# A two-layer diffusion step on one core: 43 lo halves of the first feed-forward's weights made by adding transfers, and three modulation units moved from TensorE to VectorE

## The chip, the cores and the metric

The kernel runs on one core of a Trainium2 chip. The metric is the device time of one execution in microseconds (us). The kernel before was timed three times: 2304.15, 2304.75 and 2308.19 us, median 2304.75 us. A further execution was profiled.

## The reference, cut to what matters

Two groups of 128 tokens with 2048 features (a context group and a latent group, so 256 columns in all) pass through two layers with shared weights. Each layer is a mixer and a gated feed-forward, and each of these is preceded by a modulated normalisation:

```
for l in range(2):
    mod = silu(cond) @ w_ada[l] + b_ada[l]          # six vectors of 2048 per layer and group
    sh1, sc1, gt1, sh2, sc2, gt2 = split(mod, 6)
    h = rmsnorm(x, g_norm_mix[l]) * (1 + sc1) + sh1
    x = x + gt1 * mixer(h)                           # l = 0: MLA + GQA, l = 1: differential attention
    h = rmsnorm(x, g_norm_ffn[l]) * (1 + sc2) + sh2
    x = x + gt2 * ((silu(gate) * val) @ w_down)      # gate, val: width-3 convolution of h @ w_up
y = rmsnorm(x, g_final)
```

All of it is float32. `w_up` is 2048 x 11264 and `w_down` 5632 x 2048 in each layer.

## The kernel before, in words

**Products.** Features lie on partitions and the 256 tokens on columns. Each 128 x 128 block of a weight is split into a hi part (rounded to the matmul's `fp32r` format) and a lo part (what the rounding left), and so are the activations. Three matmuls per block, hi by hi, hi by lo and lo by hi, add up in PSUM (`gemm`). A weight tile `raw` of 16 blocks, 128 x 2048 and 1 MB, comes by one DMA from SyncE's queue into one of three buffers (`Weights.load`). `split` then makes its two halves: ScalarE copies a half tile (128 x 1024) to `wh` (L248) and VectorE subtracts, giving `wl` (L249). There are four buffers of each, so the splits run up to four half tiles ahead of TensorE.

**Feed-forward** (`ffn`). It runs in two halves q. Each half has 44 up products of 16 blocks (one weight tile each), whose convolution ScalarE and VectorE do out of PSUM, and then 16 down products of 22 blocks, which are added to `x` on VectorE (L843). The first three up products are made ahead of it, in `modulated`.

**Modulation units.** `w_ada[l]` is cut into units (l, j, q): layer, one of the six vectors, a quarter of 512 columns. A unit can be worked in three ways. Units of the table `ROWS` are row sums on TensorE: four 1 MB tiles `araw`, 16 matmuls of 512 columns into the PSUM tile `ada` (`sum_rows`, L110), then a copy to `am` on ScalarE, four transposes (L113) and a few small VectorE instructions (`ada_finish`). In the trace each of those float32 matmuls has two records. Units of `FEATS` are eight steps on VectorE (`feature_step`, L473): each multiplies half of a loaded `araw` by a broadcast condition row and sums it; one 1 MB load serves two steps. Units of `DEEP` are done on VectorE beside the second mixer's attention in smaller pieces (L525).

**Pacing.** `pump` is called once per product. It adds the stage's rate for rows and for features to a balance and issues steps while the balance allows. `FRATE` holds the feature steps per product in up and down, and `RLIMIT` and `FLIMIT` hold how many units of the two tables may be begun by the end of each stage (`ab`, `ffn0`, `c`, `ffn1`). The instructions then go through a scheduler that sets each engine's order; some are pinned in program order (`keep_order`).

**Stages.** The first mixer runs until about 475 us, the first feed-forward (`ffn0`) until about 1163 us, the second mixer with its output projection until about 1580 us, and then the second feed-forward. In the second mixer each of eight heads has six products and its attention; row sums sit in the middle of a product, two tiles at a time.

Of the kernel before, what the change touches and what calls it, by code (L numbers as in the profile page):

```python
# [11 lines left out]
F32 = mybir.dt.float32  # L12
# [6 lines left out]
P = 128  # L19
# [35 lines left out]
FRATE = {"up": 0.7, "down": 1.42}  # L55
# [24 lines left out]
ROWS += [(1, 2, 1), (1, 2, 2), (1, 2, 3), (1, 4, 0), (1, 3, 0)]  # L80
FEATS = [(0, 5, 1), (0, 5, 2), (0, 5, 3)]
FEATS += [(1, j, q) for j in (1, 0) for q in range(4)]
FEATS += [(1, 2, 0)]
FEATS += [(1, 5, q) for q in range(4)]
DEEP = [[(0, 3, q) for q in range(4)], [(1, 4, q) for q in range(1, 4)] + [(1, 3, q) for q in range(1, 4)]]
RLIMIT = {"ab": 16, "ffn0": 17, "c": 22, "ffn1": 22}
FLIMIT = {"ab": 0, "ffn0": 12, "c": 12, "ffn1": 16}
# [7 lines left out]
def step_kernel(ctx: ExitStack, tc: tile.TileContext, A: dict):  # L95
# [157 lines left out]
    class Weights:  # L253
# [3 lines left out]
        def __init__(self, src, nblk, per_tile, cycle=0):  # L257
            self.src, self.nblk, self.per = src, nblk, per_tile
            self.cycle = cycle
            self.at, self.blocks, self.tiles = 0, [], []  # L260
            self.half = None
            self.begun = []
            self.used = lambda: None

        def load(self, parts=1, pin=lambda i: i):
            n = self.per
            if self.cycle:
                n = min(n, self.cycle - self.at * n % (-(-self.cycle // n) * n))
            n *= self.nblk if self.per < TB else 1
            raw = T_(wpool, [P, 4, 512], "raw").rearrange("p g n -> p (g n)")  # L270
            w = n * P // parts
            for i in range(parts):
                s = slice(i * w, (i + 1) * w)
                pin(sp.dma_start(out=raw[:, s], in_=self.src[self.at, :, s]))
            self.at += 1
            return raw, n
# [4 lines left out]
        def take(self):  # L281
            return self.begun.pop(0) if self.begun else self.load()

# [20 lines left out]
        def chunk(self):  # L304
            while len(self.blocks) < self.nblk:
# [3 lines left out]
                raw, n = self.take()  # L309
                n0 = FINE if fine[0] else 8  # L310
                for lo in range(0, n, n0):
                    hi = min(lo + n0, n)
                    w = (hi - lo) * P
                    if lo % 8 == 0:
                        wh_ = T_(wpool, [P, 1024], "wh", F32R, bufs=4)
                        wl_ = T_(wpool, [P, 1024], "wl", F32R, bufs=4)
                    at = lo % 8 * P
                    wh, wl = wh_[:, at:at + w], wl_[:, at:at + w]
                    split(wh, wl, raw[:, lo * P:hi * P])
# [1181 lines left out]
    def ffn(hx, W, ready, turn, l, st):  # L1501
# [16 lines left out]
        with tc.tile_pool(name=f"ffn{l}", bufs=1) as fp, banks(f"pffn{l}") as pf:  # L1518
# [25 lines left out]
            def up(q):  # L1544
                gs = []
                for i in range(q * KQ, (q + 1) * KQ):
                    rate = 0 if i < LATE else FRATE["up"]
# [14 lines left out]
            def down(gs, q):  # L1562
# [4 lines left out]
                for c in range(KD):  # L1567
# [13 lines left out]
                    pump(0, 0 if quiet else FRATE["down"])  # L1581
                return u

            for q in range(NQ):
                gs = up(q)
# [195 lines left out]
```

## Time and profile before

| | before |
|---|---|
| three timed runs | 2304.15, 2304.75, 2308.19 us (median 2304.75) |
| profiled execution, own time | 2307.52 us |
| its span | 2305.7 us |
| TensorE busy / weight loads busy | 2275.9 / 2182.1 us |
| VectorE / ScalarE / GpSimd busy | 1885.6 / 1195.7 / 188.1 us |
| read from HBM | 609.32 MB |

Times inside the profile count from the start of the span. Busy time of TensorE overlaps from matmul to matmul, so its pace is read from the starts of successive weight loads (PEld), one per matmul. The profiled execution's own time is 1.8 us over its span and 2.8 us over the median of the timed runs.

### The profile page before, as it was taken

Reading aid. Unit: us, or ns where it says so; the run is one execution under the profiler, and the core shown is the slowest. Engines: PE = TensorE matmul, PEld = TensorE weight load, DVE = VectorE, ACT = ScalarE, POOL = GpSimd, SP = SyncE. Lnnn points to the kernel's source line nnn. Section 1 sums busy time; section 2 is a strip of 40 time slices with the busy share of each in tenths; the row PEclk is TensorE's granted clock in tenths of the full one; section 3 lists DMA queues with packets and bytes.
Section 4 is the critical chain, followed back from the end, with each engine's and each line's share of the span. In section 5 each row is a group of like instructions: output and inputs, shape, how many; then the busy total and the mean of one; then the engine's idle time right before and its main releaser. Section 6 shows DMA issues by size and latency. Waiting matters only on the chain.

```text
span 2305.7 us, 47484 instructions
## 1 busy us (share of the span) xinstructions
PE 2275.9 (99%) x19496; PEld 2182.1 (95%) x19496; DVE 1885.6 (82%) x2973; ACT 1195.7 (52%) x1959; POOL 188.1 (8%) x238
## 2 busy tenths in 40 slices
PE   8999999999999999999999999999999999999998
PEld 6788878999999999999999999999999999999998
DVE  4667979989999999999978988898899965666654
ACT  4345555665553355555575455457555434555543
POOL 0002111300000000001130001023000000000011
PEclk9999999999999999999999999999999999999999
DMA  9987888777777777777788888776667755555553
GB/s 376 367 343 293 326 311 338 288 277 264 262 255 291 291 272 260 272 258 258 288 293 293 318 322 310 267 268 229 246 256 262 264 200 189 199 191 194 198 189 126
DMA packets 100122, 617.15 MB, mean 268 GB/s; under 512 B 10752, under 2 KB 18880, under 8 KB 33344
## 3 DMA queue, kind: packets, MB, share of 16 engines
q1 hardware_dynamic: 99904, 614.11, 72.2%
q8 instruction: 153, 2.51, 0.4%
q14 instruction: 65, 0.53, 0.1%
HBM read 609.32 MB, written 4.75 MB: 266 GB/s over the span
## 4 chain that ended last, share of the span: by engine, by line
PE 93%; DVE 3%; DMA 2%; issue 1%; POOL 1%; ACT 1%; SPq 0%; DVEq 0%; ACTq 0%; POOLq 0%
PE acc L110 86%; PE ada L110 3%; PE att L110 2%; DVE wl L249 1%; DVE hx L525 1%; DMA more<-w_ada 1%; PE att L113 1%; DMA raw<-w_out_c 0%; PE misc L110 0%; DMA araw<-w_ada 0%; DMA kvb<-w_ada 0%; POOL dev L807 0%; PE ada L113 0%; DVE rope L858 0%; ACT wh L248 0%
## 5 line engine op out<-in xcount | busy, mean ns | idle before, releaser
L110 PE MATMUL acc<-hx,wh 128*128 128x256 f32 (+1 forms) x7264 | 1255.2, 278 | 4.2 <-ACT wh L248 1.7
L248 ACT CAST wh<-raw 128x1024 fp32r<-128x1024 f32 (+1 forms) x834 | 796.6, 967 | 869.8 <-PE acc L110 736.6
L249 DVE TENSOR_TENSOR wl<-raw,wh 128x1024 fp32r<-128x1024 f32 (+1 forms) x834 | 925.4, 1126 | 246.9 <-ACT wh L248 240.2
L110 PEld LDWEIGHTS acc<-hx,wh 128*128 128x128 f32 x7264 | 1099.8, 188 | 23.2 <-ACT wh L248 8.1
L110 PE MATMUL acc<-hx,wl 128*128 128x256 f32 (+1 forms) x3632 | 1007.8, 278 | 5.3 <-DVE wl L249 5.1
L110 PEld LDWEIGHTS acc<-hx,wl 128*128 128x128 f32 x3632 | 684.5, 188 | 9.5 <-DVE wl L249 6.9
L110 PE MATMUL acc<-g,wh 128*128 128x256 f32 x2816 | 478.8, 276 | 0.0
L110 PEld LDWEIGHTS acc<-g,wh 128*128 128x128 f32 x2816 | 424.0, 188 | 0.0
L110 PE MATMUL acc<-g,wl 128*128 128x256 f32 x1408 | 388.1, 276 | 0.0
L473 DVE CUSTOM_DVE_ANT_0 junk<-araw,condb 128x2048 f32<-128x2048 f32 x128 | 294.4, 2300 | 0.0
L110 PEld LDWEIGHTS acc<-g,wl 128*128 128x128 f32 x1408 | 264.2, 188 | 0.0
L211 POOL TENSOR_TENSOR sqacc<-sqacc,sq 128x256 f32<-128x256 f32 x62 | 71.5, 1154 | 1491.1 <-ACT sq L207 1490.9
L110 PE MATMUL acc<-hxc,wh 128*128 128x256 f32 (+1 forms) x1056 | 189.3, 281 | 0.0
L110 PEld LDWEIGHTS acc<-hxc,wh 128*128 128x128 f32 x1056 | 161.9, 188 | 1.8 <-issue 1.7
L110 PE MATMUL acc<-hxc,wl 128*128 128x256 f32 (+1 forms) x528 | 146.9, 278 | 0.0
L110 PEld LDWEIGHTS acc<-hxc,wl 128*128 128x128 f32 x528 | 99.6, 189 | 0.2
L110 PE MATMUL acc<-wh,hxc 128*128 128x256 f32 (+1 forms) x512 | 95.0, 283 | 0.5 <-DVE nt L818 0.5
L1531 ACT ACTIVATE cv<-acc,convw 128x256 f32<-128x256 f32 x169 | 94.1, 557 | 0.0
L525 DVE CUSTOM_DVE_ANT_0 hx<-block,condb 128x1024 fp32r<-128x1024 f32 x65 | 79.3, 1221 | 7.3 <-DMA block<-w_ada 6.8
L1537 DVE SCALAR_TENSOR_TENSOR cv<-acc,convw,cv 128x254 f32<-128x254 f32 x169 | 81.1, 480 | 3.2
L843 DVE SCALAR_TENSOR_TENSOR x<-acc,mod,x 128x128 f32<-128x128 f32 x190 | 57.3, 344 | 31.6 <-PE acc L110 31.6
L110 PEld LDWEIGHTS acc<-wh,hxc 128*128 128x128 f32 x512 | 79.4, 188 | 3.4 <-issue 2.5
(263 smaller groups left out, 1800.4 us busy)
## 6 DMA issues: line engine op xcount, KB each, us to landing
raw<-w_up SPq DMA_DIRECT2D x176, 1024.0 KB, 4.8
araw<-w_ada SPq DMA_DIRECT2D x136, 1024.0 KB, 6.0
raw<-w_down SPq DMA_DIRECT2D x88, 1024.0 KB, 4.8
raw<-w_in_c SPq DMA_DIRECT2D x48, 1024.0 KB, 6.9
block<-w_ada SPq DMA_DIRECT2D x41, 512.0 KB, 6.8
raw<-w_in_ab SPq DMA_DIRECT2D x18, 1024.0 KB, 9.1
raw<-w_out_ab SPq DMA_DIRECT2D x16, 1024.0 KB, 7.9
raw<-w_out_c SPq DMA_DIRECT2D x16, 1024.0 KB, 7.1
```

The costliest lines, as they stand in the source:

```text
L110: return self.placed(nc.tensor.matmul(*a, **kw))
L113: return self.placed(nc.tensor.transpose(*a, **kw))
L211: eng.tensor_tensor(out=st["acc"], in0=st["acc"], in1=sq, op=ALU.add)
L248: pin(act.copy(out_hi, src))
L249: pin(dve.tensor_tensor(out=out_lo, in0=src, in1=out_hi.bitcast(F32), op=ALU.subtract))
L473: keep_order(dve.tensor_tensor_reduce(out=T_(feat["pool"], [P, D], "junk"), in1=feat["row"][:, c], in0=feat["raw"].rearrange("p g n -> p ( ...
L525: keep_order(dve.tensor_tensor_reduce(out=self.junk, in0=self.raw, in1=self.row[:, c].rearrange("p (g n) -> p g n", g=2), scale=1.0, scala ...
L843: dve.scalar_tensor_tensor(out=x[:, c, s], in0=ps[:, s], scalar=mod[:, l, 3 * which + 2, c, g:g + 1], in1=x[:, c, s], op0=ALU.mult, op1=AL ...
L1531: pin(act.activation(y, ps, AF.Identity, scale=cw[:, 1, m:m + 1], bias=cw[:, 3, m:m + 1]))
L1537: pin(dve.scalar_tensor_tensor(out=y3[:, :, :T - 1], in0=p3[:, :, 1:], scalar=cw[:, 2, m:m + 1], in1=y3[:, :, :T - 1], op0=ALU.mult, op1=A ...
```

## The change

Three `ROWS` units, (1, 2, 1), (1, 2, 2) and (1, 2, 3), become `FEATS` units, and `FLIMIT["ffn0"]` goes from 12 to 15, so that all three are worked in `ffn0`. `FRATE` becomes a list per layer, with higher rates for layer 0. In `ffn0`, `go_far` names a stretch of tiles for the up and the down weights of each q. `prepare`, called for each tile taken there, keeps two further tiles loaded and, where the tile's number leaves 1 or 3 when divided by 5, makes its second half at once in buffers of its own, two of each kind: ScalarE writes `farh` (hi) and `farl` = -hi, and GpSimd issues a DMA that adds the same 512 KB of the weight from HBM onto `farl`. No VectorE subtraction is made for such a half.

```diff
-FRATE = {"up": 0.7, "down": 1.42}
+FRATE = [{"up": 0.9, "down": 1.8}, {"up": 0.7, "down": 1.42}]
+LEAD = (9, 3)
-ROWS += [(1, 2, 1), (1, 2, 2), (1, 2, 3), (1, 4, 0), (1, 3, 0)]
+ROWS += [(1, 4, 0), (1, 3, 0)]
-FEATS += [(1, 2, 0)]
+FEATS += [(1, 2, q) for q in range(4)]
-RLIMIT = {"ab": 16, "ffn0": 17, "c": 22, "ffn1": 22}
-FLIMIT = {"ab": 0, "ffn0": 12, "c": 12, "ffn1": 16}
+RLIMIT = {"ab": 16, "ffn0": 17, "c": 19, "ffn1": 19}
+FLIMIT = {"ab": 0, "ffn0": 15, "c": 15, "ffn1": 19}
...
+        def go_far(self, home, start, stop, last):
+            self.far, self.until = home, stop
+            self.span = range(start, last)
+
+        def prepare(self):
+            while len(self.begun) < 2 and self.at < self.until:
+                self.begun.append(self.load())
+            for raw, n in self.begun:
+                i = next(i for r, i in self.index if r is raw)
+                if i in self.span and i % 5 in (1, 3) and not any(m[0] is raw for m in self.made):
+                    wh = T_(self.far, [P, 1024], "farh", F32R, bufs=2)
+                    wl = T_(self.far, [P, 1024], "farl", F32R, bufs=2)
+                    act.copy(wh, raw[:, 8 * P:n * P])
+                    act.activation(wl, wh.bitcast(F32), AF.Copy, scale=-1.0)
+                    pool.dma_start(out=wl, in_=self.src[i, :, 8 * P:n * P], accum_op=ALU.add)
+                    self.made.append((raw, wh, wl))
...
+                if self.far:
+                    self.prepare()
+                made = [m[1:] for m in self.made if m[0] is raw]
...
+                    if made and lo == 8:
+                        wh, wl = wh_, wl_ = made[0]
+                    else:
...
             for q in range(NQ):
+                if l == 0:
+                    at, n = 2 * KQ * q, KQ * KD // TB
+                    W.go_far(fp, at + LEAD[q], at + 2 * KQ, at + 2 * KQ)
+                    WD.go_far(fp, n * q + 3, n * q + n, n * q + n - 6 * q)
```

In the order of the changed program GpSimd's queue has 43 such transfers: 14 for the up and 8 for the down weights of the first half of `ffn0`, 16 and 5 for the second. On VectorE the feature steps in these four stretches go from 28, 19, 32 and 17 to 35, 26, 40 and 19.

The first place is TensorE in the second mixer, in the middle of a v product of a middle head. `acc` are the two PSUM tiles of the product, `ada` the one of the row sums. Before:

```order
L110 MATMUL acc_16556<-wh_16560,hxc_14392 128x256
L110 MATMUL acc_16557<-wh_16560,hxc_14392 128x256
L110 MATMUL acc_16557<-wl_16561,hxc_14392 128x256
L110 MATMUL acc_16557<-wh_16560,hxc_14392 128x256
L110 MATMUL ada_16183<-araw_16192,condw_79 32x512 x4
L110 MATMUL ada_16183<-araw_16297,condw_79 32x512 x4
L110 MATMUL acc_16556<-wh_16564,hxc_14392 128x256
L110 MATMUL acc_16556<-wl_16565,hxc_14392 128x256
```

And the same place in the changed program:

```order
L111 MATMUL acc_16658<-wh_16662,hxc_14510 128x256
L111 MATMUL acc_16659<-wh_16662,hxc_14510 128x256
L111 MATMUL acc_16659<-wl_16663,hxc_14510 128x256
L111 MATMUL acc_16659<-wh_16662,hxc_14510 128x256
L111 MATMUL acc_16658<-wh_16666,hxc_14510 128x256
L111 MATMUL acc_16658<-wl_16667,hxc_14510 128x256
```

The two rows of row sums are gone and the product goes on. Six such pairs of rows (48 matmuls) and three rows of four transposes leave TensorE's order after the first pumped unit, and no matmul joins it; elsewhere only the operands `wh` and `wl` of some become `farh` and `farl`.

The second place is ScalarE in `ffn0`, among the up products. `cv<-acc` empties the PSUM tile of a product, `wh<-raw` is the hi part of a half tile. Before:

```order
L248 CAST wh_6835<-raw_6833 128x1024
L248 CAST wh_6839<-raw_6833 128x1024
L1531 ACTIVATE cv_6755<-acc_6706,convw_2384 128x256
L248 CAST g_6693<-cv_6687 128x256
L248 CAST wh_6898<-raw_6896 128x1024
L1553 ACTIVATE cv_6755<-cv_6755 128x256
L248 CAST wh_6902<-raw_6896 128x1024
```

The changed program:

```order
L1557 ACTIVATE cv_6844<-acc_6795,convw_2384 128x256
L249 CAST wh_7000<-raw_6855 128x1024
L249 CAST wh_7063<-raw_6922 128x1024
L1557 ACTIVATE cv_6914<-acc_6865,convw_2384 128x256
L249 CAST g_6852<-cv_6844 128x256
L299 CAST farh_6991<-raw_6989 128x1024
L249 CAST wh_7067<-raw_6922 128x1024
L300 ACTIVATE farl_6992<-farh_6991 128x1024
```

The hi part and its negative for the second half of a later tile stand between the halves of the tile before it. TensorE's order uses `farl_6992` in the second half of product `acc_7140`, which comes after `acc_6865`, `acc_6928`, `acc_7004` and `acc_7071`. Over the 43 the product in question is most often the fourth after the last one emptied ahead of the negation, and at the least the third.

The third place is GpSimd's queue at the passage from the modulation of `ffn0` (`hx`, `block`) to what follows. Before:

```order
L807 TENSOR_SCALAR block_5444<-block_5444,scl_78,mod_77 128x128 x2
L811 TENSOR_TENSOR hx_5342<-block_5433,hx_5342 128x256
L811 TENSOR_TENSOR hx_5342<-block_5444,hx_5342 128x256
L211 TENSOR_TENSOR sqacc_12789<-sqacc_12789,sq_12878 128x256
L211 TENSOR_TENSOR sqacc_12789<-sqacc_12789,sq_12976 128x256
```

The changed program:

```order
L833 TENSOR_SCALAR block_5444<-block_5444,scl_78,mod_77 128x128 x2
L837 TENSOR_TENSOR hx_5342<-block_5433,hx_5342 128x256
L837 TENSOR_TENSOR hx_5342<-block_5444,hx_5342 128x256
L301 DMA farl_5957<-w_up 128x1024
L301 DMA farl_6099<-w_up 128x1024
```

The queue, which had nothing between the modulation and the sums of squares (`sqacc`) of the last down products, now holds the adding transfers there, 39 of them ahead of the first `sqacc` and the last four among those.

More of the change, by code (lines that the diff above doesn't have):

```diff
@@ L274, in load @@
                 pin(sp.dma_start(out=raw[:, s], in_=self.src[self.at, :, s]))
+            self.index.append((raw, self.at))
             self.at += 1
@@ L1546, in up @@
                 for i in range(q * KQ, (q + 1) * KQ):
-                    rate = 0 if i < LATE else FRATE["up"]
+                    rate = 0 if i < LATE else FRATE[l]["up"]
                     fine[0] = False
```

15 lines of the change are left out of this document (8 added, 7 removed).

## The prediction

> **What bounds the kernel now.** I read the page's busy times and chain first, then the chain in order of time, then the busy times by stage.
>
> ```profile
> PE 2275.9 (99%) x19496; PEld 2182.1 (95%) x19496; DVE 1885.6 (82%) x2973; ACT 1195.7 (52%) x1959; POOL 188.1 (8%) x238
> PE 93%; DVE 3%; DMA 2%; issue 1%; POOL 1%; ACT 1%; SPq 0%; DVEq 0%; ACTq 0%; POOLq 0%
> 474.80 690.47 PE acc L110 x6090
> ```
>
> TensorE sets the time: 93% of the chain is its own work, and the third row says that all of `ffn0` is one unbroken piece of 6090 matmuls, 690.47 / 6090 = 0.1134 us each. A product of 16 blocks (48 matmuls) is thus 5.44 us. Time is won here only by taking instructions off TensorE, and anything that makes it wait in `ffn0` is lost in full. The stages (columns: stretch, its length, busy us and instructions of each engine, granted clock, DMA share, GB/s):
>
> ```profile
> 475.00:600.00 125.00, 125.00 (x1104) 125.00 (x1103) 112.57 (x149) 70.25 (x96) 0.00 (x0) 1.00 0.70 251
> 600.00:722.00 122.00, 122.00 (x1079) 122.00 (x1078) 112.42 (x141) 60.34 (x78) 0.00 (x0) 1.00 0.72 266
> 722.00:842.00 120.00, 120.00 (x1062) 120.00 (x1060) 111.19 (x135) 50.88 (x56) 0.00 (x0) 1.00 0.79 294
> 842.00:1070.00 228.00, 228.00 (x2014) 228.00 (x2013) 210.61 (x278) 122.00 (x173) 1.59 (x2) 1.00 0.71 257
> 1070.00:1163.00 93.00, 93.00 (x823) 93.00 (x822) 91.42 (x129) 48.16 (x85) 15.96 (x13) 1.00 0.79 286
> 1300.00:1350.00 50.00, 50.00 (x421) 46.58 (x420) 46.85 (x77) 24.89 (x48) 4.86 (x6) 1.00 0.85 309
> 1350.00:1400.00 50.00, 50.00 (x419) 47.91 (x416) 38.59 (x65) 25.27 (x44) 2.33 (x4) 1.00 0.85 319
> 1400.00:1450.00 50.00, 50.00 (x427) 48.17 (x426) 46.07 (x85) 27.31 (x54) 4.17 (x6) 1.00 0.85 305
> 1450.00:1510.00 60.00, 58.97 (x487) 54.66 (x487) 49.89 (x95) 30.07 (x66) 7.24 (x9) 1.00 0.71 259
> ```
>
> VectorE is nearly as full as TensorE: in the five rows of `ffn0` it is idle for 688.0 - 638.2 = 49.8 us, in the first half's down products (722 to 842) for 8.8 us, in the last ones (1070 to 1163) for 1.6 us. So the three units don't fit there unless VectorE is given room, which is what the 43 halves do.
>
> **What is taken off TensorE.** The weight loads around one pair of row sums, in the middle of a v product, and the matmuls around one group of transposes:
>
> ```profile
> 1387.25 0.19 PEld L110 LDWEIGHTS acc<-wh,hxc 128*128 128x128 f32 x1
> 1387.56 0.16 PEld L110 LDWEIGHTS ada<-araw,condw 128*32 128x32 f32 x8
> 1388.02 0.13 PEld L110 LDWEIGHTS ada<-araw,condw 128*32 128x32 f32 x4 [0.30 <-issue]
> 1388.45 0.13 PEld L110 LDWEIGHTS ada<-araw,condw 128*32 128x32 f32 x4 [0.30 <-issue]
> 1389.42 0.19 PEld L110 LDWEIGHTS acc<-wh,hxc 128*128 128x128 f32 x1 [0.84 <-issue]
> 1434.31 0.60 PE L113 MATMUL ada<-cst,am 128*128 128x128 f32 x4
> 1434.74 1.48 PE L110 MATMUL att<-dk,dq 128*128 128x128 f32 x8
> L110 PEld LDWEIGHTS ada<-araw,condw x160: 106/109/110, 1172.3 to 1504.9; 128*32 128x32 f32 x160
> ```
>
> From the last load of the product to its next one are 2.17 us where 0.11 would do, so a pair costs 2.06 us, and four transposes cost 0.43 us. The last row has 160 loads in this stage, 16 for a pair: ten pairs, five units. The first unit is worked inside `modulated`, and the change only puts another in its place, the second is pumped as before, and six pairs and three groups of transposes go: 6 x 2.06 + 3 x 0.43 = **13.7 us**.
>
> What is late next there is VectorE, whose work in the second mixer stays. In the four late windows TensorE loses 4.1, 2.5, 2.5 and 4.5 us, and VectorE was idle for 3.2, 11.4, 3.9 and 10.1. Only the first goes below nothing, by about 1 us, and such a deficit is first drawn from the splits, which run ahead:
>
> ```profile
> ACT wh L248 <- PE acc L110: 100.6, 69, 3.7
> DVE on L1459 <- POOL var L1457: 7.6, 7, 3.0
> DVE drec L1428 <- ACT p L875: 6.8, 6, 1.8
> DVE hx L525 <- DMA more<-w_ada: 5.6, 4, 2.9
> ```
>
> These are waits between 1200 and 1510 us. ScalarE waited 69 times for TensorE to free a `wh`: all four half tiles were ready, 4 x 2.72 = 10.9 us of stock. Against that, part of VectorE's idle time is its own waits for the softmax and for pieces of `w_ada`, some 20 us, and cannot be filled. The bounds are 0 (the stock covers everything) and 6.6 us (the first and third window give back all they lose). I take 1.5 us, near the lower end, because of the 69 waits.
>
> **What is added in ffn0.** Costs from the groups of 500 to 720 us:
>
> ```profile
> L249 DVE TENSOR_TENSOR wl<-raw,wh 128x1024 fp32r<-128x1024 f32 x81 | 97.2, 1222 | 13.2 <-ACT wh L248 12.8
> L248 ACT CAST wh<-raw 128x1024 fp32r<-128x1024 f32 x82 | 86.4, 1055 | 107.5 <-PE acc L110 91.2 <-ACT g L248 12.4 <-issue 3.9
> L473 DVE CUSTOM_DVE_ANT_0 junk<-araw,condb 128x2048 f32<-128x2048 f32 x30 | 68.7, 2291 | 0.0
> L473 DVE DVE_READ_ACCUMULATOR2_ANT mod<- 128x1 f32 x30 | 4.3, 142 | 0.0
> ```
>
> VectorE gets 3 x 8 = 24 steps of 2.43 us (58.4) and loses 43 subtractions of 1.22 us (52.5): +5.9 us of 49.8. By stretch, with the counts of the order: up of the first half +7 steps, -14 subtractions, 0; its down +7, -8, **+7.2 us of 8.8**; up of the second half +8, -16, 0; its down +2, -5, -1.2. It fits everywhere, tightly in the first down. ScalarE gets 43 negations, bounded by a cast: 45 us of its 336 idle ones. Its PSUM emptying is delayed by one such instruction at most, with three PSUM tiles in turn. Cost on the path: nothing, and if VectorE's cover were gone, the 7.2 us of the first down.
>
> The trace has no adding transfer. The nearest rows for its duration are loads:
>
> ```profile
> raw<-w_up SPq DMA_DIRECT2D x176, 1024.0 KB, 4.8
> raw<-w_in_ab SPq DMA_DIRECT2D x2, 512.0 KB, 15.3
> ```
>
> 1 MB of `w_up` lands after 4.8 us, and the slowest row of the page, 512 KB in a full queue at the start, takes 15.3. The room: TensorE mostly uses `farl` in the second half of the fourth product after the one emptied last before the negation, 3.5 x 5.44 = 19.0 us later, of which ScalarE spends some 4.1 (emptying 0.6, the cast of g 0.4, three half tiles at 1.05); so 15 us are left, in the shortest case 9.5. From the nearest row, w_up's, I take about 5 us, hidden, cost 0; the other end stands under the first rival. GpSimd's queue holds nothing else until the sums of squares, and the twelve `w_ada` loads only move to an earlier stage of SyncE's queue.
>
> **Sum.** 13.7 - 1.5 + 0 = 12.2 us off. The profiled execution, 2307.52 us (span 2305.7), would become 2295.3; against the median of the runs, 2304.75, that is **2292.5, say 2293 us**.
>
> **The rivals.**
>
> (a) *The adding transfers land late*, on the other side. If one takes L us instead of the 15 there are, TensorE stands in the middle of a product, and the later splits only refill their four buffers meanwhile, so nothing is caught up: (L - 15) x 43. The gain is gone at L = 15 + 12.2 / 43 = 15.3 us, by chance what the slowest row above shows; at 16 us the time is 2293 + 43 = 2336. For it: such a transfer reads the target as well as the weight and is queued by GpSimd, and no row shows either. Against it: 5 us would have to become three times as many, on engines that are busy for 0.70 to 0.79.
>
> (b) *DMA is full in the first down.* There 294 GB/s take a share of 0.79, so 372 would fill it. The change brings 7 steps (3.5 loads, 3.7 MB) and 8 transfers (4.2 MB) into 120 us: 360 GB/s if a transfer counts once, 395 if the read of its target counts as much again. The second is 6% too much, 7.4 us, giving 2300. The other stretches stay below 355 even then. [...]
>
> (c) *GpSimd holds up VectorE* while it makes the transfers. The two do get in each other's way beside the sums of squares:
>
> ```profile
> L211 POOL TENSOR_TENSOR sqacc<-sqacc,sq 128x256 f32<-128x256 f32 x62 | 71.5, 1154 | 1491.1 <-ACT sq L207 1490.9
> L249 DVE TENSOR_TENSOR wl<-raw,wh 128x1024 fp32r<-128x1024 f32 x20 | 27.2, 1379 | 0.0
> ```
>
> The second row is from 1075 to 1160 us, where GpSimd works: 1379 ns against 1222. If each issue stopped VectorE for a `sqacc`'s 1.15 us, the stretches would get 16, 9, 18 and 6 us more, over their idle time by about 8, 1 and 3 in the last three: 12 us, back at 2305. [...]
>
> (d) *VectorE sets the second mixer* once the row sums are gone: the upper bound of 6.6 us, so a gain of 7.1 and 2298.
>
> That the change doesn't do what it says is excluded by the order of the instructions.
>
> **How the numbers follow.** Forecast 0.60; (a) 0.18, since only its price is large; (b) 0.08, (c) 0.06, (d) 0.08. A measurement of this kernel can tell about 0.2% from no change, 4.6 us, so faster means below 2300.1. The forecast and most of (d) lie there (0.66), (b), (c) and the rest of (d) are within it or just at its edge (0.13), and (a) with the worse ends of (b) and (c) is slower (0.21). The forecast's own range is 2290 (no give-back, 13.7 off, and a little scatter) to 2298. The range reaches from 2289 over (d), (b) and (c) to 2310, where only the late part of (a) and a little below are left out.
>
> **What would show it.** In the changed profile: the ten pairs of `ada` loads from 1172 to 1505 us become four, and the second mixer with its output projection is 12 us shorter; `ffn0` stays one piece of `acc` of about 690 us; TensorE has no wait for a DMA of `farl`, and that DMA lands in under 9.5 us; VectorE is busy for some 95% of `ffn0` and its `wl` keeps 1222 ns before 1070 us. A wait of PEld for `farl`, or for `raw` in the first down, would make (a) or (b) right; gaps before `wl` in the second mixer (d).

## The result, and the profile after

The changed kernel is **slower**: 2323.97 us (median of four runs, 2320.66 to 2326.57) against 2304.82 for the kernel before, timed beside it; the ratio is 1.0079, 95% interval 1.0062 to 1.0097. The forecast was 2293.0, and 2310.0 was the upper end of its range. The profiled execution took 2326.57 us, its span is 2324.8.

From the page of the changed kernel the busy times and the shares of the chain by engine, and from its chain in order of time the pieces of `ffn0`:

```profile
PE 2292.3 (99%) x19388; PEld 2209.0 (95%) x19388; DVE 1888.9 (81%) x2975; ACT 1231.6 (53%) x1999; POOL 227.8 (10%) x281
PE 94%; DVE 2%; DMA 2%; POOL 1%; ACT 1%; issue 0%; SPq 0%; DVEq 0%; ACTq 0%; POOLq 0%
```

```profile
473.16 205.57 PE acc L111 x1749
678.73 11.17 DMA farl<-w_up
689.95 505.71 PE acc L111 x4265
```

TensorE has 108 instructions less and is busy for 16.4 us more. The chain shows why: 505.71 / 4265 = 0.1186 us for each matmul, where the one piece of before had 0.1134. Only one DMA stands in the chain of `ffn0`, for the 11.17 us from its issue to its landing; TensorE stood still for 2.5 of them. The same is seen by stretch (columns as in the prediction); here the number of weight loads in a stretch of fixed length is what counts:

```profile
475.00:600.00 125.00, 125.00 (x1070) 125.00 (x1069) 110.22 (x144) 76.50 (x101) 7.13 (x8) 1.00 0.89 296
600.00:722.00 122.00, 119.81 (x1000) 119.58 (x999) 104.62 (x135) 64.37 (x84) 6.90 (x8) 0.99 0.87 292
722.00:842.00 120.00, 120.00 (x1018) 120.00 (x1017) 110.12 (x130) 52.72 (x55) 6.06 (x7) 1.00 0.94 333
842.00:1070.00 228.00, 228.00 (x1931) 228.00 (x1930) 204.14 (x263) 128.83 (x177) 12.98 (x15) 1.00 0.91 310
1070.00:1163.00 93.00, 93.00 (x790) 93.00 (x789) 89.66 (x120) 50.12 (x80) 17.65 (x15) 1.00 0.90 312
1520.00:1570.00 50.00, 50.00 (x427) 50.00 (x427) 50.00 (x84) 28.92 (x51) 14.98 (x10) 1.00 0.69 241
```

TensorE is busy without a gap in four of the five rows of `ffn0` at a granted clock of 1.00, and yet it does 3 to 4% less in these: 1930 loads in 228 us are 118.1 ns apart, 2013 before were 113.3. A busy share of 100% hid the loss. The last row is from the output projection behind the second mixer; there too 427 loads stand where the kernel before had 443:

```profile
1520.00:1570.00 50.00, 50.00 (x444) 50.00 (x443) 47.85 (x89) 29.83 (x60) 10.84 (x10) 1.00 0.69 237
```

The weight loads at the first use of a far half, some rows left out (start, duration, then the instruction; each row of `wh` or `farh` starts a block of three loads):

```profile
504.90 0.30 PEld L111 LDWEIGHTS acc<-hx,wh 128*128 128x128 f32 x2
505.24 0.30 PEld L111 LDWEIGHTS acc<-hx,wh 128*128 128x128 f32 x2
505.58 0.30 PEld L111 LDWEIGHTS acc<-hx,farh 128*128 128x128 f32 x2
505.93 0.31 PEld L111 LDWEIGHTS acc<-hx,farh 128*128 128x128 f32 x2
506.29 0.31 PEld L111 LDWEIGHTS acc<-hx,farh 128*128 128x128 f32 x2
...
508.09 0.31 PEld L111 LDWEIGHTS acc<-hx,farh 128*128 128x128 f32 x2
508.45 0.31 PEld L111 LDWEIGHTS acc<-hx,wh 128*128 128x128 f32 x2
...
511.98 0.19 PEld L111 LDWEIGHTS acc<-hx,wh 128*128 128x128 f32 x1
```

A block takes 0.34 us (113.3 ns a load) up to 505.58, then 0.36 (120 ns) while `farh` and `farl` are loaded; and when `wh` and `wl` follow, it does not go back: 511.98 - 508.45 = 3.53 us for ten blocks, 117.7 ns a load. That slow pace lasts to the end of `ffn0` (93.00 / 789 = 117.9 ns in the last stretch). In the second mixer both paces occur: right behind the kernel's pairs of wider matmuls (`PUSH`) it is the fast one 9 times out of 14, and the output projection is slow again (50.00 / 427 = 117.1 ns).

To compare kernels, three numbers are read from the starts of weight loads. **ffn0** is the stretch from the last load for the moving operand `u` (the last up product made ahead, in `modulated`) to the last for `g` (its second down products); **second mixer** goes from there to the last load for `hxc`, which is the same place ahead of the second feed-forward. In `ffn0`, a gap over 0.25 us counts as a **wait** (less 0.113), and the **pace** is the mean of all other gaps, some 6200. The numbers come from one profiled execution of each kernel, whose own time lies up to 4.3 us from the median of its runs (e6), so differences of two or three us between them can be scatter.

| | before | after | difference |
|---|---|---|---|
| ffn0, us | 702.4 | 734.4 | +32.0 |
| of it waits, us (number) | 0 | 2.5 (1) | +2.5 |
| pace, ns | 113.36 | 118.13 | 6195 x 4.77 ns = +29.5 |
| second mixer, us | 433.2 | 422.1 | -11.1 |
| all else, us | 1170.1 | 1168.3 | -1.8 |
| span, us | 2305.7 | 2324.8 | +19.1 |

Of the 1.8 us, 1.6 lie ahead of `ffn0`, whose start, 458.6 us here and 460.2 before, scatters between 457.9 and 460.8 in the profiles of this study (all but e3's).

### The profile page after: what moved, and what is told of

Same layout as the page of the kernel before. It is cut to its first block, busy times and chain, and to the rows that moved or that the text cites. A ratio compares the mean times of both kernels' runs of the same rounds, so it can differ in the third digit from the quotient of the medians.

```text
span 2324.8 us, 47335 instructions
## 1 busy us (share of the span) xinstructions
PE 2292.3 (99%) x19388; PEld 2209.0 (95%) x19388; DVE 1888.9 (81%) x2975; ACT 1231.6 (53%) x1999; POOL 227.8 (10%) x281
## 3 DMA queue, kind: packets, MB, share of 16 engines
q0 software_dynamic: 6192, 22.55, 5.3%
## 4 chain that ended last, share of the span: by engine, by line
PE 94%; DVE 2%; DMA 2%; POOL 1%; ACT 1%; issue 0%; SPq 0%; DVEq 0%; ACTq 0%; POOLq 0%
PE acc L111 89%; PE ada L111 3%; PE att L111 2%; DMA kvb<-w_ada 1%; DVE wl L250 1%; PE att L114 1%; DMA farl<-w_up 0%; PE misc L111 0%; DMA araw<-w_ada 0%; POOL dev L833 0%; DVE hx L551 0%; PE ada L114 0%; DVE x L1668 0%; POOL hxc L837 0%; ACT wh L249 0%
## 5 line engine op out<-in xcount | busy, mean ns | idle before, releaser
L111 PE MATMUL acc<-hx,wh 128*128 128x256 f32 (+1 forms) x6784 | 1188.8, 280 | 5.2 <-ACT wh L249 1.7
L249 ACT CAST wh<-raw 128x1024 fp32r<-128x1024 f32 (+2 forms) x791 | 749.7, 961 | 765.7 <-PE acc L111 637.4
L250 DVE TENSOR_TENSOR wl<-raw,wh 128x1024 fp32r<-128x1024 f32 (+2 forms) x791 | 876.3, 1121 | 264.6 <-ACT wh L249 260.8
L111 PEld LDWEIGHTS acc<-hx,wh 128*128 128x128 f32 x6784 | 1032.8, 189 | 24.0 <-issue 8.5
L111 PE MATMUL acc<-hx,wl 128*128 128x256 f32 (+1 forms) x3392 | 946.0, 279 | 4.7 <-DVE wl L250 4.4
L111 PEld LDWEIGHTS acc<-hx,wl 128*128 128x128 f32 x3392 | 639.5, 189 | 8.1 <-DVE wl L250 6.3
L111 PEld LDWEIGHTS acc<-g,wh 128*128 128x128 f32 x2608 | 396.6, 189 | 0.0
L499 DVE CUSTOM_DVE_ANT_0 junk<-araw,condb 128x2048 f32<-128x2048 f32 x152 | 349.5, 2299 | 1.3 <-DMA araw<-w_ada 1.3
L111 PE MATMUL acc<-hx,farh 128*128 128x256 f32 x480 | 88.6, 285 | 0.0
L551 DVE CUSTOM_DVE_ANT_0 hx<-block,condb 128x1024 fp32r<-128x1024 f32 x65 | 79.4, 1222 | 6.8 <-DMA block<-w_ada 6.3
L1563 DVE SCALAR_TENSOR_TENSOR cv<-acc,convw,cv 128x254 f32<-128x254 f32 x169 | 81.1, 480 | 3.5
L1560 DVE SCALAR_TENSOR_TENSOR cv<-acc,convw,cv 128x254 f32<-128x254 f32 x169 | 80.5, 477 | 3.3 <-ACT cv L1557 3.3
```

The lines of the kernel that those rows point to most:

```text
L111: return self.placed(nc.tensor.matmul(*a, **kw))
L249: pin(act.copy(out_hi, src))
L250: pin(dve.tensor_tensor(out=out_lo, in0=src, in1=out_hi.bitcast(F32), op=ALU.subtract))
L499: keep_order(dve.tensor_tensor_reduce(out=T_(feat["pool"], [P, D], "junk"), in1=feat["row"][:, c], in0=feat["raw"].rearrange("p g n -> p ( ...
L551: keep_order(dve.tensor_tensor_reduce(out=self.junk, in0=self.raw, in1=self.row[:, c].rearrange("p (g n) -> p g n", g=2), scale=1.0, scala ...
L1560: pin(dve.scalar_tensor_tensor(out=y3[:, :, 1:], in0=p3[:, :, :T - 1], scalar=cw[:, 0, m:m + 1], in1=y3[:, :, 1:], op0=ALU.mult, op1=ALU.add))
```

## The experiments

No experiment leaves out anything of the reference. "Before" in an edit means the tables and rates of the kernel before; ratios are to runs of that kernel on the same chip. After each the numbers of the table above are given as ffn0 / waits / pace / second mixer. The theory: TensorE's pace is lost through the **place** of the new buffers, beside waits. The rivals: the adding transfers land late; VectorE has no room for the steps.

### The place of the far buffers

**e2_fardve.** The tables of before, and the 43 half tiles in far buffers, but made by VectorE as all others; no adding transfer.

```diff
-                    act.activation(wl, wh.bitcast(F32), AF.Copy, scale=-1.0)
-                    pool.dma_start(out=wl, in_=self.src[i, :, 8 * P:n * P], accum_op=ALU.add)
+                    dve.tensor_tensor(out=wl, in0=raw[:, 8 * P:n * P], in1=wh.bitcast(F32), op=ALU.subtract)
```

> The changed kernel with the units, limits and rates of before, and the lo parts in the far buffers made by VectorE, with no adding transfer at all; buffers unpadded. Place theory: 120 ns while they are read, 118 elsewhere in ffn0, 27 us more there and 3 more in the second mixer's output projection, 2332 to 2336 us. Transfer theory: 113.3 ns and 2305.

Measured: 2333.85 us, ratio 1.0124 (1.0108 to 1.0139); 730.4 us / none / 117.9 ns / 433.0 us. Without a unit moved, without a transfer and without one wait, `ffn0` loses 28.0 us.

**e2b_fardve_pad64.** The same with 64 bytes left free ahead of the far buffers.

```diff
+                    if not self.made:
+                        T_(self.far, [P, 16], "farpad", bufs=1)
                     wh = T_(self.far, [P, 1024], "farh", F32R, bufs=2)
```

> The kernel before with its own units and tables, its 43 half tiles in the new buffers but made by VectorE as all others, and 64 bytes left free ahead of these buffers. Beside the run without the 64 bytes (2333.9 us) it changes nothing but their place. Theory (the place alone takes the time): weight loads from farh and farl follow each other after 113 to 114 ns in place of 120, the products around them too, ffn0 takes 702 to 704 us in place of 730, and the time is that of the kernel before, 2303 to 2308 us. Rival (the use of other buffers, or the order that they give the splits, takes it): ffn0 stays above 720 us and the time above 2325.

Measured: 2305.62 us, ratio 1.0001 (0.9991 to 1.0010); 702.4 / none / 113.4 / 432.0. The first far half of this run, at the same point of the program:

```profile
505.17 0.30 PEld L111 LDWEIGHTS acc<-hx,wh 128*128 128x128 f32 x2
505.51 0.30 PEld L111 LDWEIGHTS acc<-hx,farh 128*128 128x128 f32 x2
505.85 0.30 PEld L111 LDWEIGHTS acc<-hx,farh 128*128 128x128 f32 x2
...
508.23 0.30 PEld L111 LDWEIGHTS acc<-hx,wh 128*128 128x128 f32 x2
508.57 0.30 PEld L111 LDWEIGHTS acc<-hx,wh 128*128 128x128 f32 x2
```

Every block takes 0.34 us. By stretch, one row without the 64 bytes (e2) and one with them:

```profile
842.00:1070.00 228.00, 228.00 (x1931) 228.00 (x1930) 202.30 (x265) 115.71 (x162) 0.00 (x0) 1.00 0.68 249
842.00:1070.00 228.00, 228.00 (x2014) 228.00 (x2013) 210.58 (x276) 120.54 (x171) 2.71 (x2) 1.00 0.71 261
```

All 28 us were the place, and nothing else about the far buffers, filled by VectorE, costs anything that can be measured. In the compiled programs `farh` and `farl` start at bytes 212608, 216704, 220800 and 224896 of a partition in the changed kernel, all 128 above a multiple of 512, and so do the moving operands `hx` (27264) and `g` (from 151168). `wh` and `wl` (from 104128) are at 192, 64 bytes off, and so are the far buffers with the 64 bytes free.

**e3_beforepad.** The converse: the kernel before with the pad ahead of `wh` and `wl` cut from 192 to 128 bytes. Those are then at 128 like `hx`, and all that lies behind them, `g` too, at 64.

```diff
-T_(wpool, [P, 48], "pad", bufs=1)
+T_(wpool, [P, 32], "pad", bufs=1)
```

> The kernel before with the first pad of the weight pool 64 bytes smaller, so that wh and wl lie at 128 of each 512 bytes, as hx does; g and hxc move along to 64. No far buffers, no adding transfers. Place theory, with the distance between the two operands deciding: up products at 120 ns (27 us more in each feed-forward), down products at 113 or, if the pace isn't regained, 118 (10 more each), some 2360 to 2385 us. Transfer theory: 2305.

Measured: 2370.69 us, ratio 1.0284 (1.0267 to 1.0302); 729.4 / none / 117.7 / 437.8. Its first stretch of up products:

```profile
475.00:600.00 125.00, 125.00 (x1044) 125.00 (x1043) 108.00 (x143) 67.75 (x95) 0.00 (x0) 1.00 0.68 249
```

125.00 / 1043 = 119.8 ns. Split by operand, products of `hx` go at 120.0 to 120.2 ns and those of `g`, which is now 64 bytes off, at 113.4 in both halves. So in these runs it is the distance of the stationary from the moving operand that counts, and equal places cost 6.7 ns a load. Here no slow pace stays behind: the first products of `g` after those of `hx` already go at 113.4. Only distances of 0 and 64 bytes were tried; what others would cost was not shown.

### The change with one or both cures

**e1_pad64.** The change, with the 64 bytes of e2b.

> The changed kernel with 64 bytes of pad ahead of the far buffers, nothing else moved. In its trace weight loads follow each other after 113.3 ns until the first use of farh, after 120 while farh and farl are read, and after 118 in all products behind it, with one wait of 2.6 us in ffn0. Place theory: farh and farl lie at 128 of each 512 bytes of a partition, as the moving operands hx and g do, while wh and wl lie at 192; loads from there are slow, and the lost pace isn't regained. Then the pad gives 113 to 114 ns in ffn0 and 2294 to 2299 us. Transfer theory: the adding transfers themselves (their traffic, or TensorE's waits for them) set the pace; then it stays at 118 and the time at 2324.

Measured: 2320.26 us, ratio 1.0069 (1.0054 to 1.0084); 729.2 / 9.4 us in 7 waits / 116.2 / 419.2. Up to 637 us all loads, the far ones too, follow each other after 113 to 114 ns, but the time comes back only by 3.7 us. Then the first waits came, for `wl` and for `farl`, and the pace was the slow one from 638 to 854 us (120.00 / 1020 = 117.6 ns from 722 to 842 us) and again from 976 us to the end (93.00 / 791 = 117.6 from 1070 to 1163); in between, behind a wait of 0.65 us for `farl`, it was the fast one. The second mixer gains 14.0 us here, for its output projection keeps the fast pace:

```profile
1520.00:1570.00 50.00, 50.00 (x443) 50.00 (x443) 50.00 (x91) 27.79 (x52) 11.86 (x9) 1.00 0.69 240
```

**e6_push.** The change without the 64 bytes; in the product after each far one two matmuls are 32 and 16 columns wider, as the kernel has them behind each attention (the table `PUSH`, 13 matmuls from the first to the last).

```diff
+            W.fresh -= W.fresh > 0
+            if W.fresh == 0 and W.due:
+                push[:] = PUSH
+            W.due = W.fresh > 0
+            return gemm(blocks, xh, xl, wider=wide)
```

> The changed kernel, unpadded, with the first matmul of the product after each far one made 32 columns wider and its thirteenth 16 wider, as is done behind the attention of a head. If the slow pace is a state that stays after the far product, and a wider matmul ends it: far halves at 120 ns, the rest of ffn0 at 113.3, 27 us less than the changed kernel, less some 5 us for the 43 far halves (24 matmuls by 6.7 ns each is 7 us) and 1 for the wider ones, so about 2303 us. If the transfers slow TensorE all along, 2324 or a little more.

Measured: 2316.57 us, ratio 1.0049 (1.0030 to 1.0068); 728.8 / 10.1 us in 9 / 116.0 / 422.5. Behind 36 of the 40 pairs of wider matmuls in `ffn0` the pace is the fast one; far loads stay at 120 ns, and with TensorE at 116.0 ns there are nine waits, where the changed kernel at 118.1 had one.

**e7_padpush.** Both cures.

> The changed kernel with both: 64 bytes of pad ahead of the far buffers, and the wider matmuls in the product after each far one. The padded kernel ran at 113.3 ns until TensorE's first wait in ffn0 (at 638 us, for a late wl, then at 653 for a late farl) and at 118 from there to the end of ffn0, which took 729 us against 702 before. Theory: of the 27 us, 8 to 10 are the waits themselves (transfers that land late), the rest the slow pace that they leave behind; so with the pushes ffn0 takes 712 to 716 us, the second mixer 419 to 420, the whole 2302 to 2306. Rival, that the transfers slow every matmul while they run: 729 stays, 2318 or more.

Measured: 2308.51 us, ratio 1.0020 (1.0009 to 1.0031); 716.6 / 9.1 us in 8 / 114.2 / 419.9. What is left is mostly waits, by the view of waits for the weight loads from 475 to 1180 us (total, times, longest):

```profile
PEld acc L111 <- DMA farl<-w_up: 6.6, 5, 2.8
PEld acc L111 <- DMA farl<-w_down: 1.5, 2, 0.9
PEld acc L111 <- DVE wl L250: 0.4, 1, 0.4
```

**e9_all_push.** The 64 bytes, and the two wider matmuls in every second product of `ffn0`.

```diff
+            if l == 0 and W.count % 2 == 0:
+                push[:] = PUSH
```

> The whole change with the 64 bytes ahead of the far buffers, and every second product of ffn0 (not only those behind far halves) begins with the two wider matmuls. The run that widened only behind far halves took 2308.5 us with ffn0 at 716.6. Theory: what is left there is half slow pace behind waits for wl and farl, half those waits: ffn0 709 to 713 us, the time 2301 to 2305 us. Rival (only the waits for the adding transfers are left): unchanged, 2307 to 2310 us.

Measured: 2314.98 us, ratio 1.0043 (1.0031 to 1.0056); 721.8 / 11.2 us in 9 / 114.7 / 422.1. A miss: more widening was worse than e7. The pace makes 3.0 us of the difference, the waits 2.1 and the second mixer 2.2, where the output projection is at the slow pace again. A widening isn't free, as the next group shows (0.08 us each, e10); why the waits and the output projection differ was not followed up.

### Transfers and units apart

**e5_addalone.** The adding transfers alone, with the 64 bytes; units and rates of before.

> The adding transfers alone, in padded buffers, with the units, limits and rates of before. DMA moves 12.6 MB less in ffn0 than in the padded kernel and VectorE is idle for 100 us there. If the transfers land late because DMA is full (share 0.87 to 0.94 in ffn0), most waits vanish at about 0.84: 2305 to 2310. If they are late because of how they are issued (GpSimd's queue, ScalarE's order), the waits and the slow pace behind them stay: 2325 to 2332.

Measured: 2331.57 us, ratio 1.0112 (1.0095 to 1.0129); 727.9 / 17.5 us in 12 / 114.7 / 432.4. Six of the waits, 11.5 us, are for far halves, with VectorE under less load than before and DMA at shares of 0.85 to 0.93. The transfers are late by themselves. The other six, 6.0 us, are for `wl` and `wh`, although VectorE had less to do; ScalarE stood ahead of `farh` for a tile `raw` 38 times, 123.6 us in all (32 times and 63.2 in the changed kernel), and whether the near halves behind it in its order are late through this was not tried.

**e4_units.** Units and rates of the change, no far halves.

> The units' part alone: three units on VectorE in ffn0 with the changed rates and limits, no far halves. By busy times VectorE gets 58 us where it has 50 idle, 17 in each down stretch against 9 and 2. Theory that the second mixer gains the row sums' full price: 419 to 420 us there against 433. In ffn0 TensorE waits some 10 us for wl from the first down on, and each wait leaves the slow pace behind (4.8 ns on some 3500 matmuls, 17 us): 2312 to 2322. If VectorE's overload is taken up by the splits' stock, 2291.

Measured: 2314.72 us, ratio 1.0038 (1.0025 to 1.0051); 717.2 / 9.5 us in 10 / 114.2 / 424.9. The second mixer gains only 8.3 us here; its output projection is at the slow pace (426 loads from 1520 to 1570 us).

**e4b_twounits.** Two units moved (`FLIMIT["ffn0"]` 14, `RLIMIT["c"]` 20, rates 0.9 and 1.42), no far halves.

> Two units moved instead of three, no far halves, all added steps in the up products (0.9 a product there, 1.42 in down as before). VectorE gets 39 us in the up stretches, where it has 39 idle. If the splits' stock carries that: 9 us less than before, 2296. If TensorE waits for wl even a few times, the slow pace follows and the time is 2305 to 2320.

Measured: 2314.76 us, ratio 1.0043 (1.0028 to 1.0058); 719.4 / 2.0 us in 6 / 115.8 / 423.6. Six waits of 2.0 us in all, and 17.0 us are lost.

**e11_two_push** and **e13_two_push6.** The two units with wider matmuls in every second product of `ffn0` (54 of them), and only in the six in which or right behind which e4b had waited.

```diff
+            if l == 0 and W.count in ((29, 32) if W is WD else (17, 27, 63, 73)):
+                push[:] = PUSH
```

Of e11:

> Two units moved without far halves, as in the run that took 2314.8 us, and every second product of ffn0 begins with the two wider matmuls. Theory (slow pace behind small waits took most of its 17 us in ffn0): ffn0 falls from 719 to 704 to 709 us and the time to 2300 to 2305 us. Rival (the waits of TensorE for VectorE's splits themselves took it): ffn0 stays at 715 us or more and the time above 2310.

Of e13:

> Two units moved without far halves, and the two wider matmuls only in the six products of ffn0 in which or right behind which TensorE had waited 0.3 to 0.7 us. Theory: the waits themselves stay (2.6 us), the pace behind them is mended at once, the 64 regular widenings (5 us) are gone: ffn0 705.5 to 708 us, the second mixer 9.6 us shorter, the time 2298 to 2302 us. Rival (only regular widening holds the pace, other causes than these waits disturb it): ffn0 at 711 us or more, the time 2305 or more.

Measured: e11 2303.98 us, ratio 0.9994 (0.9985 to 1.0003); 709.1 / 2.0 us in 6 / 114.1 / 423.6. e13 2300.85 us, ratio 0.9977 (0.9967 to 0.9987); 705.5 / 2.2 us in 6 / 113.5 / 423.8. The waits are the same in all three runs; of the 17.0 us of e4b, 2.42 ns x 6190 = 15.0 are pace. Two stretches, first of e4b and then of e13, where there is no widening in the first and two in the second:

```profile
655.00:842.00 187.00, 187.00 (x1590) 187.00 (x1589) 173.11 (x210) 78.84 (x89) 0.00 (x0) 1.00 0.74 276
842.00:1030.00 188.00, 188.00 (x1597) 187.88 (x1596) 179.80 (x228) 95.11 (x133) 0.00 (x0) 1.00 0.74 271
```

```profile
655.00:842.00 187.00, 187.00 (x1652) 187.00 (x1651) 179.36 (x219) 83.36 (x96) 0.00 (x0) 1.00 0.77 287
842.00:1030.00 188.00, 187.89 (x1654) 187.55 (x1654) 184.24 (x235) 98.92 (x137) 0.00 (x0) 1.00 0.76 279
```

187.00 / 1589 = 117.7 ns, 187.00 / 1651 = 113.3. One wait of 0.3 us at 651 us left the slow pace for 385 us in e4b, which is 14 us of its loss; in e13, behind the same wait and the two wider matmuls that follow it, the pace is the fast one.

**e10_one_push** and **e12_one.** One unit moved (`FLIMIT["ffn0"]` 13, `RLIMIT["c"]` 21, rates 0.8 and 1.42), no far halves, with and without the wider matmuls in every second product.

Of e10:

> The kernel before with only one unit moved to ffn0 (up rate 0.8), no far halves, and in ffn0 every second product begins with the wider matmuls (32 and 16 columns more) that the kernel uses behind attention. Theory (a wait costs mostly the slow pace that it leaves behind, and wider matmuls end it): the second mixer gains 4.5 us, ffn0 takes 703 to 705 us, the time is 2300 to 2303 us, faster than before. Rival (VectorE has no room for eight more row steps, and the waits themselves take what is won): ffn0 above 707 us, the time 2305 or more.

Of e12:

> The kernel before with one unit moved to ffn0 and nothing else: no far halves, no widening added. With the 64 regular widenings ffn0 took 707.3 us (702.4 before) with one wait of 0.8 us at its end. Theory (those widenings cost 5 us by themselves, one unit fits): ffn0 702.5 to 704 us, the second mixer 428, the time 2299 to 2302 us, faster than before. Rival (the eight row steps cost it): ffn0 at 706 us or more, the time 2304 or more.

Measured: e10 2307.12 us, ratio 1.0008 (0.9999 to 1.0017); 707.3 / 0.6 us in 1 / 114.1 / 428.0. e12 **2300.55 us, ratio 0.9980 (0.9971 to 0.9989)**; 702.4 / none / 113.4 / 428.3. One unit fits into VectorE's idle time for nothing. The widenings cost e10 4.3 us for 54 (not 64, as the expectations have it): 0.08 us each, where the pace was fast already.

### Fewer transfers

**e14_light** and **e15_light_nopush.** Two units with the tables of e4b, far halves only where the tile's number leaves 1 when divided by 5 (22 transfers), the 64 bytes; with the widening of e7 and without it.

```diff
-                if i in self.span and i % 5 in (1, 3) and not any(m[0] is raw for m in self.made):
+                if i in self.span and i % 5 == 1 and not any(m[0] is raw for m in self.made):
```

Of e14:

> Two units moved, only every fifth tile with a far half (22 adding transfers in place of 43), the 64 bytes left free, and the wider matmuls only in products behind far halves. Theory A (the transfers land late because they come two in a row through one queue beside full traffic): with half of them TensorE waits for none or one of them, ffn0 703 to 707 us, the time 2296 to 2300 us. Theory B (each lands late by itself where the loads are dense): the waits go down by half only, ffn0 708 to 712 us, the time 2301 to 2306 us.

Of e15:

> The run with two units and 22 adding transfers (2299.5 us) without its widenings in ffn0. Theory (a widening costs 0.08 us, 22 of them 1.8, and nothing disturbs the pace there): ffn0 702.4 us, the same as before, the time 2296 to 2299 us. Rival (something besides waits lowers the pace, and the widenings mended it): ffn0 at 706 us or more, the time 2301 or more.

Measured: e14 2299.50 us, ratio 0.9975 (0.9966 to 0.9984); 704.2 / none / 113.6 / 423.6. e15 **2298.22 us, ratio 0.9970 (0.9958 to 0.9982)**; 702.9 / 0.5 us in 1 / 113.4 / 423.6: the lowest median of all, though its interval overlaps those of e12, e13 and e14. Leaving out 22 widenings gives 1.8 us of pace, 0.08 each as before. The transfers of e14 land like this, from issue, shortest, median and longest:

```profile
DMA to landing us min/median/max: 5.5/8.4/10.6
```

The median is the same as with 43; only the longest is shorter (12.1 in the changed kernel). The room from issue to first use is 10.4 to 16.7 us, and each transfer lands in its own, with 1.6 us to spare at the least.

**e16_light_three** and **e17_three_rate18.** All three units with 22 transfers and the 64 bytes, no widening; the rate of the down products 1.6 and 1.8.

Of e16:

> All three units of the change with 22 adding transfers in place of 43, the 64 bytes left free, no widening, the rate of the down products at 1.6. VectorE gets 58.4 us more in ffn0 and 26.9 less: 31.5 of its 49.8 idle ones; one unit alone (19.4) made no wait there, two without transfers (38.9) made six and lost 17 us. Theory A (TensorE waits little, fast pace holds): ffn0 702 to 706 us, the second mixer 11 to 14 us shorter, the time 2292 to 2298 us. Theory B (waits for wl come, the slow pace stays behind one of them): ffn0 710 to 720 us, the time 2301 to 2312 us.

Of e17:

> As the run with three units and 22 adding transfers, with the change's own rate of 1.8 in the down products. Theory A (the remainder at the end of ffn0 was that run's loss): no wait of 6.6 us at the end of ffn0, ffn0 703 to 706 us, the second mixer 11 us or more shorter than before, the time 2293 to 2299 us. Theory B (three units need the 43 transfers' room): waits for wl in the down products with slow pace behind them, the time 2302 us or more.

Measured: e16 2305.23 us, ratio 1.0007 (0.9992 to 1.0022); 703.4 / 0.7 us in 2 / 113.4 / 429.6. At that rate two of VectorE's steps were left over for the end of `ffn0`, and TensorE stood for 6.4 us there, with a granted clock of 0.80 from 1155 to 1180 us (1.00 before); it lost the gain in that place and says nothing on the units. e17 2301.57 us, ratio 0.9989 (0.9977 to 1.0002); 708.3 / 4.4 us in 3 / 113.6 / 419.1. Three units wait for ScalarE's and VectorE's halves, and the gain of the mixer, 14.1 us, is given back in part. Its twelve times fall into two groups, 2296.1 to 2299.4 and 2303.8 to 2310.3; the profile is from the first, and what the others do otherwise was not seen.

## Why the prediction was wrong, point by point

**What is taken off TensorE: right.** The weight loads of the row sums in the second mixer of the changed kernel, and below them its `wl` steps of 500 to 720 us:

```profile
L111 PEld LDWEIGHTS ada<-araw,condw 128*32 128x32 f32 x64 | 1.7, 108 | 3.0 <-issue 2.0 <-DMA araw<-w_ada 0.5
L250 DVE TENSOR_TENSOR wl<-raw,wh 128x1024 fp32r<-128x1024 f32 x62 | 75.2, 1222 | 22.1 <-ACT wh L249 22.0
```

64 loads are four pairs, as forecast. The 13.7 us are measured as 14.0 (e1) and 14.1 (e17), and as 4.9 and 9.6 for one and two units; kernels with no unit moved, e3 aside, lie between 432.0 and 433.2 us there. The 1.5 us of give-back were not needed; rival (d) falls. The changed kernel got 11.1 of it, since its output projection runs at the slow pace.

**What is added in ffn0, "cost on the path: nothing": this step failed.** `ffn0` took 32.0 us more where nothing was expected. The prediction took 0.1134 us a matmul as given and asked only for waits. It did not ask where the 43 halves lie. Place alone costs 28.0 us (e2 against e2b), which is all but 4.0 of the 32.0; one wait for `farl` is 2.5 of these, and the rest is pace. The step would have failed with the place mended too: `ffn0` then still takes 26.8 us more (e1), through waits of 9.4 us and the slow pace, which lasts behind some of them. The trace of before had the two paces, right beside the rows from which the pair of row sums was priced. These are weight loads of that same v product, the first two ahead of the pair and the last two behind it:

```profile
1384.87 0.30 PEld L110 LDWEIGHTS acc<-wh,hxc 128*128 128x128 f32 x2
...
1386.91 0.30 PEld L110 LDWEIGHTS acc<-wh,hxc 128*128 128x128 f32 x2
...
1389.65 0.30 PEld L110 LDWEIGHTS acc<-wh,hxc 128*128 128x128 f32 x2
...
1394.59 0.31 PEld L110 LDWEIGHTS acc<-wh,hxc 128*128 128x128 f32 x2
```

Six blocks of three in 2.04 us are 113.3 ns a load, and after the pair fourteen in 4.94 are 117.6. The code had signs too, pads and slightly widened matmuls that serve no result; the prediction did not ask what they buy. 64 bytes of one such pad are worth 66 us (e3).

**VectorE has room: half right.** In the changed kernel nothing waits for it, but that is at the slow pace; in e1 two of the seven waits are for `wl`. And 49.8 us of idle time are not 49.8 us of room: one unit (19.4 us) fits for nothing, two (38.9) already make six waits.

**Rival (a), the transfers land late: right in its mechanism, wrong in both of its numbers.** From the views of `farl` and `farh` in the changed kernel, the landing times, and what ScalarE waited for ahead of `farh` (total, times):

```profile
DMA to landing us min/median/max: 5.3/8.4/12.1
```

```profile
  DMA raw<-w_up: 51.3, 24
  DMA raw<-w_down: 11.9, 8
```

8.4 us in the median, where 5 were taken from the nearest row. The room was counted from the moment a PSUM tile is emptied, 15 us and 9.5 in the shortest case; but ScalarE had to wait for the tile `raw` itself in 32 of the 43 cases, and from issue to first use there were 10.8 to 16.1 us, 13.6 in the median. The margin is thin enough for a few of 43 to miss it. In the changed kernel the slow pace stretches that room and there is one such wait; with the pace mended the median room is 12.1 us and there are seven, 8.6 us (e7). The price "(L - 15) x 43" took one L for all, where it is the tail that costs, and it left out the pace behind each wait.

**Rival (b), the double count: right in its factor, without the price.** DMA queues from 475 to 1180 us (packets, MB, share):

```profile
q1 hardware_dynamic: 26509, 193.03, 71.8%
q0 software_dynamic: 6192, 22.55, 17.6%
```

17.6 / 22.55 against 71.8 / 193.03: an adding transfer took 2.1 times the engines' time per byte of a load. It isn't the smaller packets: the transfers' packets of 4 KB took 359 ns in the mean, and loads' packets of 4 KB in the first 475 us of the kernel before 181. The 395 GB/s and the 7.4 us rest on counting the read of the target as much again, which was the author's assumption and is shown by no run; in its place the runs show the 2.1, and 333 GB/s at a share of 0.94 in the first down, where TensorE never waited for `raw`. The engines were fuller, at shares of 0.87 to 0.94 in the five stretches where they had been at 0.70 to 0.79, and `raw` from `w_up` landed after 7.2 us in the median in place of 4.8.

**Rival (c), GpSimd holds up VectorE: wrong.** `wl` keeps 1222 ns while GpSimd issues 43 transfers of 0.87 us: between 475 and 1070 us 19 of its 1024-column instructions overlap an issue and take 1224 ns in the mean, the other 153 take 1222.

**The parts do not add.** Place alone costs 28.0 us, transfers alone 25.5, units alone 14.8, and all together 32.0. Matmuls that were at 118 ns through one cause were not made slower by the next (117.9 ns in e2, 118.1 in the changed kernel), and a slower TensorE waited less (2.5 us in the changed kernel; 9.4 in e1 and 10.1 in e6, at 116.2 and 116.0). That is why each cure by itself gave so little (3.7 and 7.4 us) and both together 15.5. What stays open is why equal places cost time, and why some waits leave the slow pace and others don't.

## What to carry to other kernels

Read TensorE's pace from the number of weight loads in a stretch, beside its busy share, before and after; here 4% of pace over `ffn0` was 28 us, more than twice the 12.2 us that the change was to win. Give a new buffer of stationary operands the same offset to the moving operands as the old ones have (28.0 us between e2 and e2b), and look for small waits as events that change the pace behind them and not by their length (0.3 us with 385 us of slow pace behind it in e4b). Where idle time on another engine is to be filled, fill it by one unit at a time: here one unit alone gained 0.20%, two with half the transfers 0.30%, and three with all of them lost 0.79%.

## What the runs showed of the hardware that was not expected

- TensorE ran the same fp32r matmul of 256 columns at 113.3 ns (the kernel before, 842 to 1070 us) or at 117.7 (e4b, 655 to 842 us), both at a granted clock of 1.00. The kernel before kept the first through all of `ffn0` without a wait. In e4b a wait of 0.3 us at 651 us had 385 us of the slow pace behind it; another of the same length at 596 us left the fast one (434 loads in the 49.00 us from 600 to 649 us, 112.9 ns), and behind one at 1036 us it was the fast one again (80.00 / 707 = 113.2 from 1040 to 1120).
- Such a matmul took 120 ns where its stationary and its moving operand both started 128 bytes above a multiple of 512 (the far halves of the changed kernel and of e2, the products of `hx` in e3), and, outside the slow pace, 113.3 to 113.4 where the two were 64 bytes apart (the kernel before, e2b, the products of `g` in e3). In the changed kernel and in e2 the pace behind the former is the slow one (117.7 ns behind the first in the changed kernel); in e3, where the moving operand changes too, it is the fast one at once (113.4).
- Behind two matmuls that are 32 and 16 columns wider the fast pace was mostly back: 36 times out of 40 in `ffn0` (e6), 9 out of 14 in the second mixer of the changed kernel. Where TensorE had it already they cost 0.08 us together (4.3 us for 54 in e10, 1.8 for 22 in e14).
- An adding transfer of 512 KB landed in 5.3 to 12.1 us, 8.4 in the median, and took 2.1 times the DMA time per byte of a load (the 43 of the changed kernel).
